# Gathering the experts' tokens in fp32 from the plain norm, one expert and then pairs

## The chip, the cores and the metric

The kernel runs on one core of one Trainium2 chip. The metric is the device time of one execution in microseconds (us); the median of several runs is quoted. Engines are named as in the profile: PE is the matrix engine (TensorE), PEld its weight loads, DVE the vector engine, ACT the scalar engine, POOL GpSimd, and SP the engine that issues the DMAs here.

## The reference

Two decoder layers on 256 tokens of width 2048, in float32. The part that the change touches is the last one: a layer norm, and after it a mixture of eight SwiGLU experts, of which each token takes two.

```python
h = layer_norm(DN_ALPHA * h + mixed @ odd_w_out[i], odd_ln1_g[i], odd_ln1_b[i])
h = layer_norm(DN_ALPHA * h + moe_swiglu(h, odd_router[i], odd_moe_w_gu[i], odd_moe_w_down[i]),
               odd_ln2_g[i], odd_ln2_b[i])

def moe_swiglu(x, w_router, w_gu, w_down):
    ...
    top_vals, top_idx = lax.top_k(logits, TOP_K)
    top_w = jax.nn.softmax(top_vals, axis=-1)
    gates = jnp.sum(jax.nn.one_hot(top_idx, N_EXPERTS, dtype=jnp.float32) * top_w[..., None], axis=1)
    y = jnp.zeros(xt.shape, jnp.float32)
    for e in range(N_EXPERTS):
        y = y + gates[:, e:e + 1] * swiglu(xt, w_gu[e], w_down[e])
```

## The kernel before

Tokens are two tiles of 128 (t = 0, 1), channels 16 blocks of 128 (KC) or 4 blocks of 512 (NCB). A large matmul is made of three matmuls in fp32r (`mm3`, L116 to L118): a value is split into its fp32r rounding (`h`, hi) and the remainder (`l`, lo), and hi by hi, hi by lo and lo by hi are added in PSUM. Weights come in groups of 4 channel blocks, 1 MB each (`load`): SP issues the DMA into `raw` (5 buffers), ACT casts it to `wh` (L107), DVE subtracts for `wl` (L108); `wh` and `wl` have 4 buffers each. `self.plan` gives a `wl` an instruction of DVE that it has to come behind.

The matmuls of one output block are `block`/`blocks`. After each two channel blocks they call `step_fill`, which takes one entry from the list `self.fill` and issues it.

`moe` follows the output projection of the odd layer (`out_proj`), which leaves alpha * h + f(h) in `self.h[t]` and its statistics. It makes 1/std and mean (`rstd`, `nmr`), router logits, the two largest (`top2`, L782 is the selection `sel`), and a slot number for each chosen token and expert (`pos1`, L681) by a triangular matmul over `sel` (L679 to L698). A few matmuls without a use (`keep_busy`, L900) lie between.

Tile t = 0 of h is normed on DVE (`ln_apply`, L224 and L225). Tile t = 1 is normed on ACT (L659) and multiplied by g and shifted by b on DVE (L673, L674, L688, L689). Then `token_parts` splits both into `xth` (ACT, L634) and `xtl` (DVE, L635).

An expert's tokens are not indexed but gathered by a matmul with a one-hot matrix `Dt` (token by slot, 128 slots per expert, made by L809 from `pos1`). `gather` makes this for two experts at a time: in four quarters of 4 channel blocks, for the hi and then the lo part, L827 multiplies `xth` or `xtl` (the stationary operand, 128 x 128) by `Dt` (256 columns moving, fp32r), and ACT copies two blocks at a time to `xe` (L829). `slots` (L838) adds the transposed `Dt` and the gate of each slot.

For each expert `expert_up` runs six blocks of 16 channel blocks (widths 512, 512, 512, 512, 384, 384), with SwiGLU and transposes after each pair, and `expert_down` four blocks of 11 channel blocks. Each of those four is followed by the scatter back to the tokens (L886, L887, `DT`) and an add into h (`add_stats`). The first gather, of experts 0 and 1, lies ahead of expert 0. The others lie in the `expert_down` of experts 1, 3 and 5, a quarter (`step(n)`) ahead of each of the four blocks.

The tiles `xth`, `xtl`, `xe` and the rows of g and b (`load_gb`, four tiles) come from one pool of 17 buffers (`punit`, tag "unit"); small PSUM results from 4 buffers (`ps`). The order of instructions on an engine is set when the program is built, by dependencies and by the order in the source among what the builder's own model takes to be ready.

Of the kernel before, what the change touches and what calls it, by code (L numbers as in the profile page):

```python
# [10 lines left out]
F32 = mybir.dt.float32  # L11
# [3 lines left out]
AF = mybir.ActivationFunctionType  # L15
ALU = mybir.AluOpType
AX = mybir.AxisListType

P = 128
D = 2048  # L20
KC = D // P
NT = 2
CB = 512
NCB = D // CB
WINDOWS = (2, 4, 8, 16)
NEXP = 8
# [46 lines left out]
class Trunk:  # L73
# [23 lines left out]
    def load(self, src, w=CB):  # L97

        nc = self.nc
        fence = self.plan.pop(0) if self.plan else None  # L100
        src = src.rearrange("p (k n) -> p k n", n=w)
        kc = src.shape[1]
        raw = self.praw.tile([P, kc, w], F32, tag="raw", name="raw")
        wh = self.pw.tile([P, kc, w], F32R, tag="wh", name="wh")
        wl = self.pw.tile([P, kc, w], F32R, tag="wl", name="wl")
        nc.sync.dma_start(raw, src)
        nc.scalar.copy(wh, raw)  # L107
        self.after(nc.vector.tensor_tensor(wl, raw, wh.bitcast(F32), ALU.subtract), fence)  # L108
        return wh, wl, kc

    def loads(self, src, w=CB):
# [489 lines left out]
    def router_prep(self, pm):  # L601

        nc, i = self.nc, self.i
        self.gR = pm.tile([P, 2, P], F32, tag="Dt", name="gR", bufs=2)[:, 0, :].rearrange("p (k e) -> p k e", k=KC)
        tmp = self.pln.tile([P, KC * (NEXP + 2)], F32, tag="lnT", name="bR")
        bR = tmp[:, :KC * NEXP].rearrange("p (k e) -> p k e", k=KC)
        cols = tmp[:, KC * NEXP:].rearrange("p (a c) -> p a c", a=2)
        red = pm.tile([P, 2 * NEXP], F32, tag="rred", name="rred", bufs=1)
        self.rows = pm.tile([P, 2 * NEXP], F32, tag="rrows", name="rrows", bufs=1)
        nc.sync.dma_start(bR, i["odd_router"].rearrange("p (k e) -> p k e", k=KC))  # L610
        nc.sync.dma_start(cols, i["ln_cols"][:, 4 * KC:].rearrange("p (a c) -> p a c", a=2))
        for a, dst in ((0, self.gR), (1, bR)):
            nc.vector.tensor_tensor(dst, bR, cols[:, a, :].unsqueeze(2).to_broadcast([P, KC, NEXP]), ALU.mult)
            nc.vector.tensor_reduce(red[:, a * NEXP:(a + 1) * NEXP], dst.rearrange("p k e -> p e k"), AX.X, ALU.add)
        ps = self.ps()
        nc.tensor.matmul(ps[:, :2 * NEXP], self.c[:, C_ONE:C_ONE + P], red, start=True, stop=True)
        nc.vector.tensor_copy(self.rows, ps[:, :2 * NEXP])
        self.lg = [self.acc() for _ in range(NT)]
        nc.scalar.preload_act_table_set("natural_log_exp_and_others")
# [9 lines left out]
            nc.tensor.matmul(self.lg[t][:, :NEXP], rT[:, j * P:(j + 1) * P], self.gR[:, k, :],  # L629
                             start=k == 0, stop=k == KC - 1)  # L630

    def token_parts(self, src, dst, q, fence):
        cs = slice(q * CB, (q + 1) * CB)
        self.nc.scalar.copy(dst[0][:, cs], src)  # L634
        self.after(self.nc.vector.tensor_tensor(dst[1][:, cs], src, dst[0][:, cs].bitcast(F32), ALU.subtract), fence)  # L635

    def moe(self, pm, stats, G, B):
        nc, tc, i = self.nc, self.tc, self.i
        xtok = {}
        sel, pos1, gg = {}, {}, {}  # L640
# [3 lines left out]
        mm = nc.tensor.matmul  # L644
        for t in range(NT):
            gg[t] = gall[:, 0:t + 2:t + 1, :]
        for t in range(NT):
            for half in range(2):
                xtok[t, half] = (self.unit("xth", shape=[P, 1024]), self.unit("xtl", shape=[P, 1024]))
        gates = {}  # L650
        for t in range(NT):
            mean, rstd = self.rstd(stats[t])
            if t == 0:
                self.plan += [self.last]
            nmr = self.nmr(mean, rstd)
            hs = [self.h[t][:, n * CB:(n + 1) * CB] for n in range(NCB)]
            if t:
                for n in range(NCB):
                    nc.scalar.activation(hs[n], hs[n], AF.Identity, bias=nmr, scale=rstd)  # L659
            lrow = pm.tile([P, NEXP], F32, tag="lrow", name="lrow", bufs=1)  # L660
            logits = pm.tile([P, NEXP], F32, tag="logits", name="logits", bufs=1)
            nc.vector.scalar_tensor_tensor(lrow, self.rows[:, :NEXP], nmr, self.rows[:, NEXP:],
                                           ALU.mult, ALU.add)
            nc.vector.scalar_tensor_tensor(logits, self.lg[t][:, :NEXP], rstd, lrow, ALU.mult, ALU.add)
            sel[t], gates[t] = self.top2(logits)
            if t == 0:
                for n in range(NCB):
                    self.ln_apply(hs[n], mean, rstd, G[n], B[n])
                h0 = hs
        fence = self.last  # L670
        self.plan += [fence] * 3
        self.keep_busy(8, self.c[:, :CB // 2].bitcast(BF16))
        self.after(nc.vector.tensor_tensor(hs[0], hs[0], G[0], ALU.mult), fence)  # L673
        self.after(nc.vector.tensor_tensor(hs[0], hs[0], B[0], ALU.add), fence)  # L674
        for t in range(NT):
            pp = self.ps()
            if t == 1:
# [3 lines left out]
            ins = nc.vector.scalar_tensor_tensor(pos1[t], pp[:, :NEXP], 1.0, sel[t], ALU.add, ALU.mult)  # L681
            self.after(ins, fence)
        self.keep_busy(6, self.c[:, :CB // 2].bitcast(BF16))
        gat = self.gather(xtok, [pos1[t][:, 0:2] for t in range(NT)], gg, 0, 0)
        fence = self.last
        for n in range(NCB):
            if n:
                self.after(nc.vector.tensor_tensor(hs[n], hs[n], G[n], ALU.mult), fence)  # L688
                self.after(nc.vector.tensor_tensor(hs[n], hs[n], B[n], ALU.add), fence)  # L689
            self.token_parts(h0[n], xtok[0, n // 2], n % 2, fence)  # L690
            self.token_parts(hs[n], xtok[1, n // 2], n % 2, fence)
        for t in range(NT):
            gv = gg[t][:, 1, :2 * NEXP].rearrange("p (e s) -> p e s", s=2)
            nc.scalar.copy(gv[:, :, 0], gates[t])
# [7 lines left out]
        fstats = [self.stats_tile() for _ in range(NT)]  # L702
# [2 lines left out]
        gat[4]()  # L705
        for e in range(NEXP):
            cur = gat
            hT = self.expert_up(e, cur, e % 2)
            step = None
            if e % 2 and e + 1 < NEXP:  # L710
                gat = self.gather(xtok, [pos1[t][:, e + 1:e + 3] for t in range(NT)], gg, e + 1, 0)
                gat[4]()
                step = gat[3]
            self.expert_down(e, cur, e % 2, hT, e == 0, fstats if e == NEXP - 1 else None, step)

        G, B = self.load_gb(i["odd_ln2_g"], i["odd_ln2_b"])
        self.final_norm(fstats, G, B)
        most_v = nc.values_load(most[0:1, 0:1], min_val=0, max_val=2 * P)
        with tc.If(most_v > P):
# [3 lines left out]
            with tc.For_i(0, NEXP) as e:  # L723
                gat = self.gather(xtok, [pr[:, t, 0:1] for t in range(NT)], gg, 0, P, num=1)
# [3 lines left out]
                hT = self.expert_up(e, gat, 0)  # L728
# [67 lines left out]

    def gather(self, xtok, pos, gg, e, offset, num=2):

        nc, pm = self.nc, self.pm
        mm = nc.tensor.matmul  # L800
        Dt = []
# [10 lines left out]
        xe = {}  # L812
        us = {}

        def quarter(q):
            for part in range(2):
                if q % (3 - num) == 0:
                    us[part] = self.unit("xe", shape=[P, (3 - num) * 4, num * P])
                u = us[part][:, q % (3 - num) * 4:q % (3 - num) * 4 + 4, :]
                for r in range(2):  # L820
                    ps = self.ps()
                    for j in range(2):
                        o = ps[:, j * num * P:(j + 1) * num * P]
                        c = q * 4 + r * 2 + j
                        cs = slice((c % 8) * P, (c % 8 + 1) * P)
                        for t in range(NT):
                            mm(o, xtok[t, c // 8][part][:, cs], Dt[t].rearrange("p a b -> p (a b)"),  # L827
                               start=j == 0 and t == 0, stop=t == 1, skip_group_check=True)
                    nc.scalar.copy(u[:, r * 2:r * 2 + 2, :],  # L829
                                   ps[:, :2 * num * P].rearrange("p (c t) -> p c t", c=2))  # L830
                xe[q, part] = u
        DTs, gss = [], []

        def slots():
            for p in range(num):
# [9 lines left out]
                DTs.append(DT)  # L845
                gss.append(gs)
        return xe, DTs, gss, quarter, slots

    def expert_up(self, e, gat, p):
# [170 lines left out]
```

## Time and profile before

| what | value |
|---|---|
| median of 3 runs | 2180.92 us (2180.24 to 2181.5) |
| the profiled execution, its own time | 2179.94 us |
| its span in the trace | 2178.2 us |
| PE busy in the span | 2144.2 us (98%) |
| DVE, ACT busy | 1457.7 us (67%), 1146.9 us (53%) |
| last matmul of the odd output projection starts | 1336.10 us |
| first weight matmul of expert 0 starts | 1359.86 us |

Times of instructions are us from the start of the span. Matmuls are pipelined: the duration that the trace gives for one (390 ns for 512 columns) is longer than the distance from one start to the next (227 ns), and it is the distance that adds up. A row of the timeline that merges n instructions runs from the first start to the last end.

### The profile page before, as it was taken

Reading aid. Unit: us, or ns where it says so; the run is one execution under the profiler, and the core shown is the slowest. Engines: PE = TensorE matmul, PEld = TensorE weight load, DVE = VectorE, ACT = ScalarE, POOL = GpSimd, SP = SyncE. Lnnn points to the kernel's source line nnn. Section 1 sums busy time; section 2 is a strip of 40 time slices with the busy share of each in tenths; the row PEclk is TensorE's granted clock in tenths of the full one; section 3 lists DMA queues with packets and bytes.
Section 4 is the critical chain, followed back from the end, with each engine's and each line's share of the span. In section 5 each row is a group of like instructions: output and inputs, shape, how many; then the busy total and the mean of one; then the engine's idle time right before and its main releaser. Section 6 shows DMA issues by size and latency. Waiting matters only on the chain.

```text
span 2178.2 us, 24443 instructions
## 1 busy us (share of the span) xinstructions
PE 2144.2 (98%) x9956; PEld 1780.5 (82%) x9956; DVE 1457.7 (67%) x1225; ACT 1146.9 (53%) x962; POOL 1.6 (0%) x6
## 2 busy tenths in 40 slices
PE   9999999999999999999999998999999999999996
PEld 7888888888888888888788887888888888888884
DVE  5443566555455654456676457888888888888988
ACT  5445355343333333343643335766766766676664
POOL 0000000000000000000000000000000000000000
PEclk9999999999999999999999999999999999999998
DMA  9543645555464554455554543999999999998995
GB/s 354 210 155 142 238 179 210 199 195 192 158 226 157 215 191 184 184 190 196 213 193 176 212 160 118 333 351 349 334 336 362 343 338 341 349 346 321 372 353 203
DMA packets 82198, 537.80 MB, mean 247 GB/s; under 512 B 9504, under 2 KB 10656, under 8 KB 28192
## 3 DMA queue, kind: packets, MB, share of 16 engines
q1 hardware_dynamic: 82080, 536.18, 66.1%
q8 instruction: 80, 1.31, 0.2%
q14 instruction: 38, 0.31, 0.0%
HBM read 534.04 MB, written 2.10 MB: 246 GB/s over the span
## 4 chain that ended last, share of the span: by engine, by line
PE 94%; DVE 3%; ACT 1%; DMA 1%; issue 1%; SPq 0%; DVEq 0%; ACTq 0%
PE acc L117 29%; PE acc L118 29%; PE acc L116 29%; PE ps L181 2%; PE ps L827 1%; DVE wl L108 1%; PE ps L886 1%; PE ps L887 1%; ACT wh L107 1%; ACT lnT L259 0%; DMA raw<-in_odd_moe_down_dram 0%; PE ps L575 0%; PE acc L629 0%; PE ps L448 0%; DMA raw<-in_odd_moe_gu_dram 0%
## 5 line engine op out<-in xcount | busy, mean ns | idle before, releaser
L108 DVE TENSOR_TENSOR wl<-raw,wh 128x2048 fp32r<-128x2048 f32 (+2 forms) x519 | 1121.2, 2178 | 394.9 <-ACT wh L107 393.7
L107 ACT CAST wh<-raw 128x2048 fp32r<-128x2048 f32 (+2 forms) x519 | 935.2, 1824 | 444.9 <-PE acc L118 410.2
L117 PE MATMUL acc<-wl,xh 128*128 128x512 f32 x928 | 363.1, 391 | 1.1 <-DVE wl L108 1.1
L116 PE MATMUL acc<-wh,xh 128*128 128x512 f32 x928 | 361.4, 390 | 0.1
L118 PE MATMUL acc<-wh,xl 128*128 128x512 f32 x928 | 361.3, 390 | 0.0
L117 PE MATMUL acc<-wl,xe 128*128 128x512 f32 (+1 forms) x768 | 286.6, 373 | 0.1
L118 PE MATMUL acc<-wh,xe 128*128 128x512 f32 (+1 forms) x768 | 285.4, 372 | 0.0
L116 PE MATMUL acc<-wh,xe 128*128 128x512 f32 (+1 forms) x768 | 284.5, 371 | 0.0
L117 PE MATMUL acc<-wl,hTh 128*128 128x512 f32 x704 | 277.9, 395 | 0.7 <-DVE wl L108 0.6
L118 PE MATMUL acc<-wh,hTl 128*128 128x512 f32 x704 | 277.7, 394 | 0.0
L116 PE MATMUL acc<-wh,hTh 128*128 128x512 f32 x704 | 275.9, 392 | 0.0
L117 PEld LDWEIGHTS acc<-wl,xh 128*128 128x128 f32 x928 | 174.2, 188 | 37.1 <-DVE wl L108 1.5
L116 PEld LDWEIGHTS acc<-wh,xh 128*128 128x128 f32 x928 | 174.1, 188 | 37.1 <-ACT xh L174 0.5
L118 PEld LDWEIGHTS acc<-wh,xl 128*128 128x128 f32 x928 | 174.2, 188 | 36.0 <-DVE xl L175 0.2
L117 PEld LDWEIGHTS acc<-wl,xe 128*128 128x128 f32 x768 | 144.2, 188 | 21.9 <-DVE wl L108 1.8
L116 PEld LDWEIGHTS acc<-wh,xe 128*128 128x128 f32 x768 | 144.2, 188 | 20.6
L118 PEld LDWEIGHTS acc<-wh,xe 128*128 128x128 f32 x768 | 144.2, 188 | 19.8
L117 PEld LDWEIGHTS acc<-wl,hTh 128*128 128x128 f32 x704 | 132.3, 188 | 30.9 <-DVE wl L108 2.1
L116 PEld LDWEIGHTS acc<-wh,hTh 128*128 128x128 f32 x704 | 132.3, 188 | 29.6
L118 PEld LDWEIGHTS acc<-wh,hTl 128*128 128x128 f32 x704 | 132.4, 188 | 27.8
L174 ACT CAST hTh<-ps 128x512 fp32r<-128x512 f32 (+1 forms) x46 | 26.2, 569 | 181.2 <-PE ps L181 181.2
L116 PE MATMUL acc<-wh,x0h 128*128 128x512 f32 x256 | 103.7, 408 | 1.9 <-ACT wh L107 1.9
(195 smaller groups left out, 1793.2 us busy)
## 6 DMA issues: line engine op xcount, KB each, us to landing
raw<-in_odd_moe_gu_dram SPq DMA_DIRECT2D x128, 1024.0 KB, 6.4
raw<-in_even_ffn_gu_dram SPq DMA_DIRECT2D x88, 1024.0 KB, 4.8
raw<-in_odd_moe_down_dram SPq DMA_DIRECT2D x64, 1024.0 KB, 7.1
raw<-in_odd_moe_gu_dram SPq DMA_DIRECT2D x64, 768.0 KB, 5.8
raw<-in_even_ffn_down_dram SPq DMA_DIRECT2D x44, 1024.0 KB, 4.8
raw<-in_odd_w_in_dram SPq DMA_DIRECT2D x32, 1024.0 KB, 4.8
raw<-in_even_w_in_dram SPq DMA_DIRECT2D x30, 1024.0 KB, 5.3
raw<-in_odd_moe_down_dram SPq DMA_DIRECT2D x32, 768.0 KB, 6.6
```

The lines of the kernel that those rows point to most:

```text
L107: nc.scalar.copy(wh, raw)
L108: self.after(nc.vector.tensor_tensor(wl, raw, wh.bitcast(F32), ALU.subtract), fence)
L116: mm(acc, xh, wh, start=first, stop=False)
L117: mm(acc, xh, wl, start=False, stop=False)
L118: mm(acc, xl, wh, start=False, stop=last)
L174: self.nc.scalar.copy(hi, src)
L181: self.nc.tensor.transpose(ps[:, j * P:(j + 1) * P], src[:, j * P:(j + 1) * P], self.ident)
L827: mm(o, xtok[t, c // 8][part][:, cs], Dt[t].rearrange("p a b -> p (a b)"), start=j == 0 and t == 0, stop=t == 1, skip_group_check=True)
L886: nc.tensor.matmul(ps, DT[:, t, :], yh, start=True, stop=False)
L887: nc.tensor.matmul(ps, DT[:, t, :], yl, start=False, stop=True)
```

## The change

The norm writes `(h - mean) / std`, without g and b, for both token tiles by ACT into four tiles `xtok` in fp32; the split into hi and lo is gone from there. The gather multiplies these fp32 tiles by `Dt` read as fp32. Its PSUM result (now with channels on partitions) gets g as a per-partition scale and b as a bias in an ACT activation into `f`, and is split there into hi and lo. g and b as columns (`xcols`) stay from `router_prep` on.

The first gather is for expert 0 alone (`num=1`), the next ones for the pairs (1, 2), (3, 4), (5, 6), in the `expert_down` of experts 0, 2 and 4, and the last for expert 7 alone, in that of expert 6. The residual `h = xtok * g + b` is made by DVE inside `expert_up` of expert 0, as 8 entries of `self.fill`, four steps apart.

```diff
@@ load
-        self.after(nc.vector.tensor_tensor(wl, raw, wh.bitcast(F32), ALU.subtract), fence)
+        self.wl_ins = nc.vector.tensor_tensor(wl, raw, wh.bitcast(F32), ALU.subtract)
+        self.after(self.wl_ins, fence)
@@ router_prep
-        cols = tmp[:, KC * NEXP:].rearrange("p (a c) -> p a c", a=2)
+        cols = self.xcols = pm.tile([P, 2, KC], F32, tag="xcols", name="xcols", bufs=1)
@@ moe
-                xtok[t, half] = (self.unit("xth", shape=[P, 1024]), self.unit("xtl", shape=[P, 1024]))
+                xtok[t, half] = self.unit("xtok", F32, [P, 1024])
...
-            if t:
-                for n in range(NCB):
-                    nc.scalar.activation(hs[n], hs[n], AF.Identity, bias=nmr, scale=rstd)
+            for n in range(NCB):
+                nc.scalar.activation(xtok[t, n // 2][:, n % 2 * CB:(n % 2 + 1) * CB],
+                                     self.h[t][:, n * CB:(n + 1) * CB], AF.Identity, bias=nmr, scale=rstd)
...
-            if t == 0:
-                for n in range(NCB):
-                    self.ln_apply(hs[n], mean, rstd, G[n], B[n])
...
-        self.after(nc.vector.tensor_tensor(hs[0], hs[0], G[0], ALU.mult), fence)
-        self.after(nc.vector.tensor_tensor(hs[0], hs[0], B[0], ALU.add), fence)
...
-        gat = self.gather(xtok, [pos1[t][:, 0:2] for t in range(NT)], gg, 0, 0)
-        fence = self.last
+        gat = self.gather(xtok, [pos1[t][:, 0:1] for t in range(NT)], gg, 0, 0, num=1)
+
+        def residual(t, n):
+            hs = self.h[t][:, n * CB:(n + 1) * CB]
+            self.after(nc.vector.tensor_tensor(hs, xtok[t, n // 2][:, n % 2 * CB:(n % 2 + 1) * CB], G[n],
+                                               ALU.mult), self.wl_ins)
+            nc.vector.tensor_tensor(hs, hs, B[n], ALU.add)
+        self.fill = [None] * 6
         for n in range(NCB):
-            if n:
-                self.after(nc.vector.tensor_tensor(hs[n], hs[n], G[n], ALU.mult), fence)
-                self.after(nc.vector.tensor_tensor(hs[n], hs[n], B[n], ALU.add), fence)
-            self.token_parts(h0[n], xtok[0, n // 2], n % 2, fence)
-            self.token_parts(hs[n], xtok[1, n // 2], n % 2, fence)
+            for t in range(NT):
+                self.fill += [partial(residual, t, n), None, None, None]
@@ moe, the loop over experts
-            hT = self.expert_up(e, cur, e % 2)
+            p = (e + 1) % 2 if e else 0
+            hT = self.expert_up(e, cur, p)
+            while self.fill:
+                self.step_fill()
-            if e % 2 and e + 1 < NEXP:
-                gat = self.gather(xtok, [pos1[t][:, e + 1:e + 3] for t in range(NT)], gg, e + 1, 0)
+            if e % 2 == 0 and e + 1 < NEXP:
+                num = min(2, NEXP - 1 - e)
+                gat = self.gather(xtok, [pos1[t][:, e + 1:e + 1 + num] for t in range(NT)], gg, e + 1, 0, num=num)
@@ gather, quarter
+            if q % (3 - num) == 0:
+                for part in range(2):
+                    us[part] = self.unit("xe", shape=[P, (3 - num) * 4, num * P])
+            o = q % (3 - num) * 4
+            per = 4 // num
+            for r in range(num):
+                ps = self.ps().rearrange("p (c t) -> p c t", c=per)
+                f = self.pln.tile([P, per, num * P], F32, tag="lnT", name="xf")
+                for j in range(per):
+                    c = q * 4 + r * per + j
+                    cs = slice((c % 8) * P, (c % 8 + 1) * P)
+                    for t in range(NT):
+                        mm(ps[:, j, :], xtok[t, c // 8][:, cs], Dt[t].rearrange("p a b -> p (a b)").bitcast(F32),
+                           start=j == 0 and t == 0, stop=t == 1, skip_group_check=True)
+                for j in range(per):
+                    c = q * 4 + r * per + j
+                    nc.scalar.activation(f[:, j, :], ps[:, j, :], AF.Identity, bias=self.xcols[:, 1, c:c + 1],
+                                         scale=self.xcols[:, 0, c:c + 1])
+                at = slice(o + r * per, o + r * per + per)
+                self.split_evac(f, us[0][:, at, :], us[1][:, at, :])
             for part in range(2):
-                if q % (3 - num) == 0:
-                    us[part] = self.unit("xe", shape=[P, (3 - num) * 4, num * P])
-                u = us[part][:, q % (3 - num) * 4:q % (3 - num) * 4 + 4, :]
-                for r in range(2):
-                    ps = self.ps()
-                    for j in range(2):
-                        o = ps[:, j * num * P:(j + 1) * num * P]
-                        c = q * 4 + r * 2 + j
-                        cs = slice((c % 8) * P, (c % 8 + 1) * P)
-                        for t in range(NT):
-                            mm(o, xtok[t, c // 8][part][:, cs], Dt[t].rearrange("p a b -> p (a b)"),
-                               start=j == 0 and t == 0, stop=t == 1, skip_group_check=True)
-                    nc.scalar.copy(u[:, r * 2:r * 2 + 2, :],
-                                   ps[:, :2 * num * P].rearrange("p (c t) -> p c t", c=2))
-                xe[q, part] = u
+                xe[q, part] = us[part][:, o:o + 4, :]
```

## Rows read from the trace of the kernel before

**Rows 1.** Busy time by stretch: PE, PEld, DVE, ACT, POOL; PE clock, DMA share, GB/s.

```profile
1360.00:2152.00 792.00, 790.59 (x3759) 669.95 (x3758) 676.45 (x448) 558.11 (x421) 0.00 (x0) 1.00 0.92 344
...
1360.00:1400.00 40.00, 40.00 (x180) 33.06 (x179) 32.02 (x22) 29.26 (x21) 0.00 (x0) 1.00 0.90 326
1500.00:1550.00 50.00, 50.00 (x269) 44.56 (x269) 40.84 (x31) 36.95 (x37) 0.00 (x0) 1.00 0.93 349
1600.00:1650.00 50.00, 50.00 (x245) 43.78 (x244) 44.92 (x32) 34.06 (x27) 0.00 (x0) 1.00 0.96 358
```

**Rows 2.** Timeline of PE ahead of expert 0: start, length, instruction [idle before, releaser].

```profile
1336.10 0.39 PE L118 MATMUL acc<-wh,mxl 128*128 128x512 f32 x1
...
1343.18 0.37 PE L698 MATMUL ps<-sel,c 128*128 128x8 f32 x2
1345.34 2.44 PE L827 MATMUL ps<-Dt,xth 128*128 128x256 f32 x8 [1.79 <-DVE gates L794]
...
1351.72 1.22 PE L827 MATMUL ps<-Dt,xtl 128*128 128x256 f32 x4 [3.09 <-ACT xe L829]
1352.74 1.91 PE L827 MATMUL ps<-Dt,xth 128*128 128x256 f32 x8
...
1355.55 1.12 PE L827 MATMUL ps<-Dt,xth 128*128 128x256 f32 x8
...
1359.86 0.39 PE L116 MATMUL acc<-wh,xe 128*128 128x512 f32 x1
```

**Rows 3.** Matmuls on fp32r and on fp32 operands: count, duration min/median/max in ns.

```profile
L827 PE MATMUL ps<-Dt,xth x128: 277/281/582, 1345.3 to 1954.7; 128*128 128x256 f32 x128
L386 PE MATMUL ps<-qkT x16: 377/377/379, 100.5 to 173.0; 128*128 128x256 f32 x16
L408 PE MATMUL ps<-atta,v x16: 377/378/378, 110.9 to 183.2; 128*128 128x256 f32 x16
L575 PE MATMUL ps<-sguw,sguv x64: 275/275/348, 1138.5 to 1156.6; 128*128 128x128 f32 x64
```

**Rows 4.** Timeline of PE where such fp32 matmuls run, merged.

```profile
110.94 0.59 PE L408 MATMUL ps<-atta,v 128*128 128x256 f32 x2
111.37 0.39 PE L409 MATMUL ps<-atta,v 128*128 128x128 f32 x2
...
1138.49 3.81 PE L575 MATMUL ps<-sguw,sguv 128*128 128x128 f32 x32 [0.26 <-DVE sguv L225]
```

**Rows 5.** Timeline of DVE ahead of expert 0.

```profile
1342.66 0.23 DVE L782 SCALAR_TENSOR_TENSOR sel<-c,idx,oh 128x8 f32<-128x8 f32 x1
...
1343.65 0.69 DVE L674 TENSOR_TENSOR h<-h,gb 128x512 f32<-128x512 f32 x1
...
1344.33 0.15 DVE L681 SCALAR_TENSOR_TENSOR pos<-ps,sel 128x8 f32<-128x8 f32 x1
...
1344.91 0.28 DVE L809 TENSOR_SCALAR Dt<-c,pos 128x128 fp32r<-128x128 f32 x1
...
1346.23 0.69 DVE L688 TENSOR_TENSOR h<-h,gb 128x512 f32<-128x512 f32 x1
1346.84 0.68 DVE L635 TENSOR_TENSOR xtl<-h,xth 128x512 fp32r<-128x512 f32 x1
...
1353.61 2.29 DVE L108 TENSOR_TENSOR wl<-raw,wh 128x2048 fp32r<-128x2048 f32 x1
```

**Rows 6.** Busy time and granted clock in short stretches, columns as in Rows 1.

```profile
10.00:13.00 3.00, 3.00 (x8) 2.09 (x8) 2.70 (x6) 2.34 (x6) 0.00 (x0) 0.50 1.07 412
14.00:17.00 3.00, 3.00 (x15) 2.47 (x14) 2.08 (x3) 1.37 (x3) 0.00 (x0) 1.00 1.02 397
1336.00:1344.00 8.00, 6.07 (x39) 4.07 (x37) 6.57 (x34) 6.61 (x10) 0.00 (x0) 1.00 0.01 3
1348.00:1351.00 3.00, 0.63 (x3) 0.34 (x2) 3.00 (x6) 1.05 (x2) 0.00 (x0) 0.50 0.00 0
1355.00:1360.00 5.00, 5.00 (x43) 5.00 (x43) 5.00 (x4) 5.00 (x11) 0.00 (x0) 1.00 0.62 216
```

**Rows 7.** Timeline of ACT in an earlier norm: scale and bias from PSUM, then cast.

```profile
1057.28 1.83 ACT L259 ACTIVATE lnT<-ps,lncols 128x128 f32<-128x128 f32 x5
1059.00 0.63 ACT L174 CAST xh<-lnT 128x512 fp32r<-128x512 f32 x1
1059.51 1.52 ACT L259 ACTIVATE lnT<-ps,lncols 128x128 f32<-128x128 f32 x4
1060.89 0.65 ACT L174 CAST xh<-lnT 128x512 fp32r<-128x512 f32 x1
```

More of the change, by code (lines that the diff above doesn't have):

```diff
@@ L604, in router_prep @@
         self.gR = pm.tile([P, 2, P], F32, tag="Dt", name="gR", bufs=2)[:, 0, :].rearrange("p (k e) -> p k e", k=KC)
-        tmp = self.pln.tile([P, KC * (NEXP + 2)], F32, tag="lnT", name="bR")
-        bR = tmp[:, :KC * NEXP].rearrange("p (k e) -> p k e", k=KC)
-        cols = tmp[:, KC * NEXP:].rearrange("p (a c) -> p a c", a=2)
+        bR = self.pln.tile([P, KC, NEXP], F32, tag="lnT", name="bR")
+        cols = self.xcols = pm.tile([P, 2, KC], F32, tag="xcols", name="xcols", bufs=1)
         red = pm.tile([P, 2 * NEXP], F32, tag="rred", name="rred", bufs=1)
@@ L630, in router_step @@
                              start=k == 0, stop=k == KC - 1)
[L632 to L635, printed above, removed]
     def moe(self, pm, stats, G, B):
@@ L655, in moe @@
             nmr = self.nmr(mean, rstd)
-            hs = [self.h[t][:, n * CB:(n + 1) * CB] for n in range(NCB)]
-            if t:
-                for n in range(NCB):
-                    nc.scalar.activation(hs[n], hs[n], AF.Identity, bias=nmr, scale=rstd)
+            for n in range(NCB):
+                nc.scalar.activation(xtok[t, n // 2][:, n % 2 * CB:(n % 2 + 1) * CB],
+                                     self.h[t][:, n * CB:(n + 1) * CB], AF.Identity, bias=nmr, scale=rstd)
             lrow = pm.tile([P, NEXP], F32, tag="lrow", name="lrow", bufs=1)
@@ L665, in moe @@
             sel[t], gates[t] = self.top2(logits)
-            if t == 0:
-                for n in range(NCB):
-                    self.ln_apply(hs[n], mean, rstd, G[n], B[n])
-                h0 = hs
         fence = self.last
@@ L707, in moe @@
             cur = gat
-            hT = self.expert_up(e, cur, e % 2)
+            p = (e + 1) % 2 if e else 0
+            hT = self.expert_up(e, cur, p)
+            while self.fill:
+                self.step_fill()
             step = None
-            if e % 2 and e + 1 < NEXP:
-                gat = self.gather(xtok, [pos1[t][:, e + 1:e + 3] for t in range(NT)], gg, e + 1, 0)
+            if e % 2 == 0 and e + 1 < NEXP:
+                num = min(2, NEXP - 1 - e)
+                gat = self.gather(xtok, [pos1[t][:, e + 1:e + 1 + num] for t in range(NT)], gg, e + 1, 0, num=num)
                 gat[4]()
                 step = gat[3]
-            self.expert_down(e, cur, e % 2, hT, e == 0, fstats if e == NEXP - 1 else None, step)
+            self.expert_down(e, cur, p, hT, e == 0, fstats if e == NEXP - 1 else None, step)
         G, B = self.load_gb(i["odd_ln2_g"], i["odd_ln2_b"])
```

## The prediction

> **What bounds the kernel now.** The page gives PE 98% of the span, but an average over stages doesn't say what one stage is worth, so I read three views in this order. First the busy time by stretch over the experts: PE is busy 790.59 of 792 us, while DVE has 676, ACT 558, and the DMA engines a share of 0.92 [rows 1]. So in this stage PE never waits for weights: whatever PE is given to do there more adds to the time nearly one for one, and at most the 1.4 us of idle can be won back. Second the timeline of PE between the output projection and expert 0: the last matmul of the one starts at 1336.10, the first of the other at 1359.86 [rows 2]. This bridge of 23.8 us is the one place where DVE and ACT set the end. Third, inside the bridge, the order of DVE and the granted clock [rows 5, 6]. The change shortens the bridge and alters PE's work in the expert stage; I cost the two separately.
>
> **What one gather costs PE, before.** A pair has 16 channel blocks, 2 token tiles and 2 parts (hi and lo): 64 matmuls of 256 columns in fp32r. Four gathers make 4 x 32 = 128 records for the hi part, and the trace has 128 [rows 3]: one record per matmul. At full clock eight of them take 1.12 us with the last one's 0.28 us tail [rows 2], so the distance is (1.12 - 0.28) / 7 = 0.120 us. A pair costs 64 x 0.120 = 7.7 us; the three gathers inside the expert stage cost 23.0 us.
>
> **What one gather costs PE, after.** The hi and lo parts become one fp32 operand, so the number of matmuls halves to 32 for a pair. But an fp32 matmul isn't one pass here. The attention scores issue L386 once for each of 8 heads, and the trace has 16 records; L408 likewise; L575 is issued 32 times (16 blocks, 2 tiles) and has 64 [rows 3]. So each fp32 matmul runs as two records. And each record is slow by itself: two of L408 at 256 columns start at 110.94 and what follows them at 111.37 [rows 4], so one takes 0.43 / 2 = 0.215 us, against 0.120 in fp32r. At 128 columns 32 records of L575 span 3.81 us: (3.81 - 0.275) / 31 = 0.114 us. A pair in fp32 is therefore 32 x 2 x 0.215 = 13.8 us, and a single expert 32 x 2 x 0.114 = 7.3 us: as much as a pair costs now.
>
> The row shows 0.43 us for 256 columns in fp32 against 0.120 in fp32r, a factor of 3.6 for half the number of matmuls. The Trainium skill, FP8 and Floating Point Precision, section "TensorE Precision Notes", says that true fp32 takes four passes through the array; by four passes at 0.120 a pair would be an estimated 15.4 us, and the change 4.9 us dearer than I have it over three pairs. The row has the duration, so it is used. The page speaks against halving the matmuls by taking fp32, and the row agrees in direction.
>
> **The expert stage.** After: three pairs, 41.3 us, and expert 7 alone, 7.3 us: 48.6. Minus the 23.0 of before: +25.6 us. All of it stands in PE's own queue between weight matmuls, in a stage where PE has 1.4 us of idle [rows 1]. Bounds: 25.6 - 1.4 = 24 if every idle moment is recovered, and 27 if each quarter adds some tenths at its ends.
>
> The other engines in these gathers: ACT now makes, for 512 elements of a PSUM tile, two activations of 256 columns and one cast, where it made two copies. The trace has no 256-column activation with scale and bias; from above, four of 128 and a cast repeat every 1.89 us (the casts at 1059.00 and 1060.89) [rows 7], 15 us for the eight tiles of a gather; from below it is the copies of today, which are part of ACT's 36.95 of 50 us [rows 1]. I take the upper value, as the nearest row. DVE gets 8 subtractions of 0.6 us, 4.8 us, in a stretch where it has 9 of 50 us free [rows 1]. Both are spread over four blocks in which PE gets 6.1 us longer, and the next expert's `xe` is wanted only after them. Cost nothing; if ACT's ceiling did reach PE through the PSUM buffers, up to 1 us per gather.
>
> **The bridge.** Four steps, all from rows.
> 1. `pos` of tile 1 is written at 1344.33, though its matmul ended at 1343.55: DVE was in the two 0.69 us operations on h (L673, L674), which go [rows 2, 5]. With one expert there are two `Dt`, not four, 0.28 us each. First gather matmul at about 1344.2 instead of 1345.34: 1.1 us.
> 2. The 3.09 us stall [rows 2] goes. It sits where `xe` needs buffers: 8 for the split tokens, 8 for `xe` and 4 for g and b are 20 of 17, so ACT had to wait for the residual. After it is 4 + 4 + 4 = 12. The splits (8 casts, 8 subtractions) and the residual that fed them go from the bridge as well [rows 5].
> 3. The gather itself, 64 records: 7.3 us at full clock. But the clock is at half from about 1345 to 1354.5 [rows 6], and eight fp32r matmuls then take 1.91 us, 0.214 apart [rows 2]; half clock doubles the 0.114 to 0.23. How long will it be low? At the kernel's start PE was busy without a break, and a low stretch (10 to 13) was over before 14 [rows 6]; in the bridge it stayed low through a stretch in which PE was busy 0.63 of 3 us. With nothing to stall it, the new gather looks like the first case. I take 4 us low: 4 / 0.23 = 17 records, and 47 x 0.114 = 5.4: 9.4 us, to 1353.6. With the two `slots` matmuls, 0.24: expert 0 starts at 1353.8.
> 4. Evacuation: 1.9 us of ACT per quarter [rows 7] and a subtraction of 0.69. Quarter 0 is through PE by about 1347.8 and in `xe` by 1351, the last by 1357; expert 0 wants the first at 1353.8 and the last 3 x 12 x 0.227 = 8.2 us later. Hidden.
>
> Gain: 1359.86 - 1353.8 = 6.1 us. Bounds: never low, 1344.2 + 7.3 + 0.24 = 1351.7, a gain of 8.1. Low throughout, 64 x 0.23 = 14.7, gain 0.7; and the builder may put one `wl` (2.29 us, [rows 5]) into the hole that L673 and L674 leave ahead of `pos`, -2.2. So -1.5 to +8.
>
> **The residual in expert 0.** 16 operations on DVE, 0.6 us apart [rows 5], 9.6 us in the roughly 60 us of `expert_up`. DVE is busy 32 of the first 40 us there, so 8 in 40, 12 in 60, are free [rows 1]: that is the cover. Each pair of blocks queues behind the last `wl` issued, and what is behind it on DVE is the next `wl`, for which PE would wait; the weights are three groups ahead, so 1.2 or 2.4 us of delay are bridged. I put it at 0. If the cover is gone (in the fullest stretch DVE has 44.92 of 50), up to 3 us.
>
> Without effect: the norm of tile 0, which moves from DVE to ACT under the matmuls of the output projection; `xcols`; SP's queue, on which no DMA changes its place.
>
> **Sum.** Span 2178.2 + 25.6 - 6.1 = 2197.7. The profiled run's own time is 1.7 above its span, so 2199.4, and the median of the runs shown is 1.0 above that run: 2200.4 us, +0.9%.
>
> **Rivals.**
> - Faster: the gather's fp32 matmul costs one record, not two. Then the expert stage has 3 x 32 x 0.215 + 32 x 0.114 = 24.3 us for 23.0, and the bridge's gather takes about 5: expert 0 starts near 1350.5 (bounded by the first evacuation), 9 us gained: 2180.9 + 1.3 - 9 = 2173. For it: the trace of before has no fp32 matmul with this one-hot operand, which is written as fp32r and only read as fp32. Against: three different fp32 matmuls all show double records. It decides the sign where a 256-column fp32 matmul costs under about 0.27 us (3.5 x 32 x 0.27 = 30, the 23.0 of before and 7 of the bridge). 4%.
> - Faster: the weight stream is the real limit of the expert stage (DMA share 0.96, 358 GB/s in the fullest stretch [rows 1]), and the longer gathers fill waiting time. Then only the bridge counts: 2180.9 - 6.1 = 2175. Against: PE's 1.4 us idle of 792. 3%.
> - The bridge isn't shortened (low clock throughout and a `wl` in front) and the residual makes PE wait: 2180.9 + 25.6 + 0 to 1.5 + 0 to 3 = 2206.5 to 2211. For it: the order on DVE is the builder's, and the clock did stay low for 10 us. 15%.
>
> **How the numbers follow.** The forecast has 78%: 2200.4. Its own range is 24 to 27 for the stage less 8 to 1.5 for the bridge: 2197 to 2206. Taking in the lower part of the third rival, and 1 us for the idle won back: 2196 to 2208. This kernel's measurement tells 0.2% (4.4 us) from no change. Slower by more than that: forecast and third rival, 93%. Within it: 2%, a forecast in which half of the stage's cost is hidden. Faster: 5%.
>
> **What would show it.** The gather's matmul with 192 records at 256 columns and 128 at 128 columns, 0.215 and 0.114 us apart. Four quarters of 3.4 us in the `expert_down` of 0, 2 and 4. First weight matmul of expert 0 near 1353.8, and no stall on `xe`. PE idle in the expert stage still about 1 us. The prediction is wrong if the records aren't double, if PE has gaps that the gathers fill, or if DVE shows up as a releaser of weight matmuls in expert 0.

## The result, and the profile after

The changed kernel takes 2197.97 us (median; 2197.52 to 2198.81), the kernel before 2181.11 us (2180.24 to 2181.94) in the same comparison. The ratio is 1.008, its 95% interval 1.0069 to 1.009: 16.9 us slower. The span of the profiled execution grew from 2178.2 to 2195.6 us, by 17.4.

Part 1 of the page, busy time by engine:

```profile
PE 2167.0 (99%) x10019; PEld 1798.6 (82%) x10020; DVE 1475.2 (67%) x1249; ACT 1169.7 (53%) x1006; POOL 1.6 (0%) x6
```

Busy time by stretch, with columns as in [rows 1]:

```profile
1360.00:2152.00 792.00, 791.96 (x3719) 671.70 (x3718) 681.85 (x470) 570.46 (x455) 0.00 (x0) 1.00 0.90 335
1360.00:1400.00 40.00, 40.00 (x187) 33.77 (x186) 39.15 (x31) 29.76 (x20) 0.00 (x0) 1.00 0.86 312
1336.00:1344.00 8.00, 6.66 (x41) 4.59 (x40) 6.02 (x30) 7.28 (x10) 0.00 (x0) 1.00 0.01 3
1344.00:1351.00 7.00, 6.95 (x62) 6.98 (x63) 7.00 (x10) 4.82 (x13) 0.00 (x0) 1.00 0.49 183
```

In the same 792 us PE is idle for 0.04 us where it was idle for 1.4 [rows 1], and it does less: the DMA engines move 335 GB/s where they moved 344, since the weights are used more slowly. PE was the limit and still is. In the first 40 us DVE is busy 39.15 us, where it was 32.02 [rows 1]: the residual. In the last stretch, the gather, the granted clock is 1.00, where it was 0.50 [rows 6].

The timeline of PE, first the bridge, which answers [rows 2], then a quarter of a later gather and the last matmuls of all, the scatter of expert 7:

```profile
1336.75 0.39 PE L119 MATMUL acc<-wh,mxl 128*128 128x512 f32 x1
...
1344.05 7.38 PE L824 MATMUL ps<-Dt,xtok 128*128 128x128 f32 x64 [0.32 <-DVE Dt L805]
...
1351.39 0.39 PE L117 MATMUL acc<-wh,xe 128*128 128x512 f32 x1
...
1415.88 3.62 PE L824 MATMUL ps<-Dt,xtok 128*128 128x256 f32 x16
...
2175.54 0.74 PE L889 MATMUL ps<-yl,DT 128*128 128x512 f32 x2
```

In the kernel before, the scatter of expert 7 ends with this row:

```profile
2158.02 0.74 PE L887 MATMUL ps<-yl,DT 128*128 128x512 f32 x2
```

The bridge, from the last matmul of the output projection to the first weight matmul of expert 0, is now 1351.39 - 1336.75 = 14.64 us, where it was 23.76: a gain of 9.1. The gather has no break in it, and the stalls of 1.79 and 3.09 us [rows 2] are gone.

The gather's matmul as a group (count of records, duration min/median/max in ns, first and last start, then the shapes; the counts beside them, 96 and 64, are here those of the matmuls that the kernel issues), which answers [rows 3]:

```profile
L824 PE MATMUL ps<-Dt,xtok x320: 270/378/380, 1344.1 to 2069.5; 128*128 128x256 f32 x96, 128*128 128x128 f32 x64
```

There are 320 records for 160 matmuls (3 x 32 for the pairs, 2 x 32 for experts 0 and 7): two for each, at both shapes. At 256 columns 16 records span 3.62 us, so they lie (3.62 - 0.378) / 15 = 0.216 us apart; at 128 columns 64 span 7.38, so (7.38 - 0.275) / 63 = 0.113. The expert stage is taken here from the start of the first weight matmul of expert 0 to the start of the last matmul of expert 7's scatter. It is 824.5 us, where it was 798.5: it grew by 26.0 us.

DVE in the bridge and after it, which answers [rows 5]:

```profile
1342.84 0.23 DVE L777 SCALAR_TENSOR_TENSOR sel<-c,idx,oh 128x8 f32<-128x8 f32 x1
...
1343.55 0.17 DVE L669 SCALAR_TENSOR_TENSOR pos<-ps,sel 128x8 f32<-128x8 f32 x1 [0.27 <-PE ps L667]
1343.63 0.47 DVE L805 TENSOR_SCALAR Dt<-c,pos 128x128 fp32r<-128x128 f32 x2
1344.10 2.28 DVE L108 TENSOR_TENSOR wl<-raw,wh 128x2048 fp32r<-128x2048 f32 x1
1346.36 2.28 DVE L108 TENSOR_TENSOR wl<-raw,wh 128x2048 fp32r<-128x2048 f32 x1
1348.63 0.67 DVE L176 TENSOR_TENSOR xe<-xf,xe 128x512 fp32r<-128x512 f32 x1
...
1364.67 2.29 DVE L108 TENSOR_TENSOR wl<-raw,wh 128x2048 fp32r<-128x2048 f32 x1 [0.42 <-ACT wh L107]
1366.88 1.29 DVE L676 TENSOR_TENSOR h<-xtok,gb 128x512 f32<-128x512 f32 x2
1368.08 1.29 DVE L678 TENSOR_TENSOR h<-h,gb 128x512 f32<-128x512 f32 x2
1369.29 4.49 DVE L108 TENSOR_TENSOR wl<-raw,wh 128x2048 fp32r<-128x2048 f32 x2
```

`pos` of tile 1 now follows its matmul at once, and two `wl` stand directly behind `Dt`; before, the first `wl` in the bridge stood at 1353.61, behind the operations on h [rows 5]. The residual's four operations at 1366.88 lie between two `wl`, inside expert 0. The page's list of waits has PE's weight loads waiting for `wl` for 4.9 us in the whole span, where it was 6.2 us before, and PE is busy 40.00 of the first 40 us of expert 0: the residual made nobody wait.

So the sum of the trace is 26.0 - 9.1 = 16.9 us, and 0.65 us by which the output projection happened to end later (1336.75 for 1336.10): 17.5 us, where the span grew by 17.4.

### The profile page after: what moved, and what is told of

The parts are those of the page before. It is cut to its first block, busy times and chain, and to the rows that moved or that the text cites. A ratio compares the mean times of both kernels' runs of the same rounds, so it can differ in the third digit from the quotient of the medians.

```text
span 2195.6 us, 24656 instructions
## 1 busy us (share of the span) xinstructions
PE 2167.0 (99%) x10019; PEld 1798.6 (82%) x10020; DVE 1475.2 (67%) x1249; ACT 1169.7 (53%) x1006; POOL 1.6 (0%) x6
## 4 chain that ended last, share of the span: by engine, by line
PE 96%; DVE 2%; ACT 1%; issue 0%; DMA 0%; SPq 0%; DVEq 0%
PE acc L118 29%; PE acc L119 29%; PE acc L117 29%; PE ps L824 3%; PE ps L182 2%; DVE wl L108 1%; PE ps L888 1%; PE ps L889 1%; ACT lnT L260 0%; PE ps L576 0%; PE ps L449 0%; PE acc L629 0%; DMA raw<-in_even_w_in_dram 0%; PE ps L399 0%; DVE h L235 0%
```

## The experiments

**Theory.** The change is two things. The bridge gets 9 us shorter because nothing in it waits for the norm's g and b any more; and each gather of a pair gets 6 us longer, because an fp32 matmul of 256 columns runs as two records of 0.216 us where the fp32r pair of matmuls took 0.120 each. **Rivals.** The longer stage comes from something else that came with the change (the odd pairing, two activations for each tile on ACT, the residual on DVE); or the shorter bridge comes from the single-expert gather alone.

**The later gathers in fp32r.** All but expert 0's gather multiply a token operand in fp32r, in as many matmuls as before. Here the high part is multiplied twice and the low part is left out, so the gathered tokens come out about doubled; the number of matmuls is that of a real split, but DVE's subtractions for a low part are not made.

```diff
+    nc.scalar.copy(self.hi[key][:, cs], xtok[key][:, cs])            # in residual
...
-    mm(ps[:, j, :], xtok[t, c // 8][:, cs], Dt[t]....bitcast(F32), ...)
+    for part in range(2):
+        mm(ps[:, j, :], hi[t, c // 8][:, cs], Dt[t]..., ...)
```

> The changed kernel with all gathers behind the first one taken back to fp32r: ACT also casts the plain norm into hi tiles inside expert 0, and a gather multiplies hi twice where hi and lo would stand (the low parts are left out of the gathered tokens, so their cost is there and their value is not). Grouping, evacuation with g and b, and residual stay. Theory (fp32 operands cost two records of 0.215 us each at 256 columns, and nothing else in the change costs PE time among the experts): each of three pairs falls from 64 x 0.215 = 13.8 to 64 x 0.120 = 7.7 us, the single stays at 7.3; 2198.0 - 18.3 = 2179.7, between 2178 and 2182. Rival (the longer evacuation on ACT and DVE, the residual, or the extra gather for expert 7 is the cost): 2192 or more.

Measured: 2179.89 us (2178.33 to 2183.18), ratio to the kernel before 0.9998 (0.9989 to 1.0008). The timeline of PE in this kernel, a pair and expert 7 alone:

```profile
1425.41 2.04 PE L836 MATMUL ps<-Dt,xth 128*128 128x256 f32 x16
...
2040.09 1.45 PE L836 MATMUL ps<-Dt,xth 128*128 128x128 f32 x12
```

The same 16 records that span 3.62 us in fp32 span 2.04 in fp32r: (2.04 - 0.280) / 15 = 0.117 us apart. The bridge is 14.64 us, as in the changed kernel, and the expert stage 806.6: 17.9 us less than in the changed kernel, and 8.1 more than before. That is the theory's number. Taken the other way: the odd pairing, ACT's activations and the residual are all still in this kernel, and together they cost 8.1 us, of which some 7.2 (64 x 0.112) is the eighth expert's own gather. So what the eighth expert's own gather costs is nearly what the bridge gives back, and the fp32 pairs are the loss.

**Pairs from expert 0 on, in fp32.** Four gathers of pairs as before, the first in the bridge again.

```diff
-    gat = self.gather(xtok, [pos1[t][:, 0:1] for t in range(NT)], gg, 0, 0, num=1)
+    gat = self.gather(xtok, [pos1[t][:, 0:2] for t in range(NT)], gg, 0, 0)
...
-    if e % 2 == 0 and e + 1 < NEXP:
+    if e % 2 and e + 1 < NEXP:
```

> The changed kernel with the grouping of before: pairs (0,1), (2,3), (4,5), (6,7), all in fp32. Theory: the gather ahead of expert 0 grows from 7.1 to 13.8 us (+6.6), the expert stage loses the gather of expert 7 alone (-7.3): 2197.3, between 2195 and 2199. Rival A (starting with one expert is what shortens the bridge, as the evacuation of a pair, up to 15 us of ACT, holds expert 0 up): 2203 or more. Rival B (the fp32 gathers among the experts are partly hidden, so that moving one ahead of expert 0 costs its full price and saves less): 2200 to 2204.

Measured: 2197.49 us, ratio 1.0078 (1.0061 to 1.0095), no different from the changed kernel. PE's timeline:

```profile
1337.21 0.39 PE L119 MATMUL acc<-wh,mxl 128*128 128x512 f32 x1
...
1344.71 14.05 PE L823 MATMUL ps<-Dt,xtok 128*128 128x256 f32 x64 [0.52 <-DVE Dt L804]
...
1359.07 0.39 PE L117 MATMUL acc<-wh,xe 128*128 128x512 f32 x1
```

A whole pair in fp32 in the bridge is 64 records in 14.05 us, against 64 in 7.38 for one expert. The bridge is 21.86 us, 7.2 longer than after, and the stage 816.6, 7.9 shorter. A gather of one expert ahead only moves 7 us from the bridge into the stage: at these two widths PE pays for fp32 by the column (0.113 us a record at 128, 0.216 at 256), and eight experts have the same columns however they are grouped. The bridge with the whole fp32 pair is only 1.9 us shorter than that of the kernel before (21.86 against 23.76). So 7.2 of the 9.1 us gained there are the second expert's gather put off to the stage, and the rival of the single expert holds for that part. The waits and the low clock that are gone pay for the dearer fp32 gather of a pair and 1.9 us more.

**The residual ahead of expert 0.** The sixteen operations of the residual are issued before expert 0, not inside it.

```diff
-    self.fill = [None] * 6
+    self.wl_ins = self.last
     for n in range(NCB):
         for t in range(NT):
-            self.fill += [partial(residual, t, n), None, None, None]
+            residual(t, n)
```

> The changed kernel with the residual made ahead of expert 0, right behind the one-hot matrices, instead of inside expert 0. Theory (inside expert 0 the residual is covered by DVE's free time and costs nothing; ahead of it, 16 x 0.6 = 9.6 us of DVE stand in front of the low weights and the low parts of the first gather): 2200 to 2206. Rival (the residual inside expert 0 makes PE wait): 2197 or less.

Measured: 2202.52 us, ratio 1.0102 (1.0085 to 1.0118), 4.6 us more than the changed kernel. PE's and DVE's timelines, then two windows:

```profile
1352.75 0.38 PE L840 MATMUL ps<-gg,Dt 128*128 128x256 f32 x1 [1.70 <-DVE gg L686]
...
1354.03 0.79 PE L119 MATMUL acc<-wh,xe 128*128 128x512 f32 x1 [0.89 <-DVE xe L176]
```

```profile
1352.69 0.68 DVE L678 TENSOR_TENSOR h<-h,gb 128x512 f32<-128x512 f32 x1
1353.29 1.29 DVE L176 TENSOR_TENSOR xe<-xf,xe 128x512 fp32r<-128x512 f32 x2
```

```profile
1350.00:1354.00 4.00, 1.43 (x9) 0.80 (x7) 4.00 (x10) 0.37 (x1) 0.00 (x0) 0.95 0.00 0
1354.00:1357.00 3.00, 2.97 (x7) 2.39 (x8) 3.00 (x4) 2.99 (x9) 0.00 (x0) 0.50 0.00 0
```

The bridge by its definition is still 14.64 us, but PE then stands: for `gg` 1.70 us, for `xe` 0.89, both behind the residual on DVE, which is busy 4.00 of 4 us while PE is busy 1.43. Behind that idle stretch the granted clock is 0.50. The stage is 829.1 us, 4.6 longer. So moving the residual is worth 4.6 us of the change, which is about half of the bridge's gain, and inside expert 0 it costs nothing. A shorter bridge as the first weight matmul shows it isn't yet a gain: one has to see that the next one follows.

**Without the filler matmuls.** The two stretches of `keep_busy` matmuls in the routing part are left out.

```diff
-    self.keep_busy(8, self.c[:, :CB // 2].bitcast(BF16))
...
-    self.keep_busy(6, self.c[:, :CB // 2].bitcast(BF16))
```

> The changed kernel without the two batches of matmuls without a use (8 and 6) between the router and the gather. Theory (they keep the clock at full, and a half clock would stretch the first gather from 7.1 us towards 14 us): 2201 to 2205, granted clock 0.5 for part of the gather. Rival (without stalls the gather itself keeps or brings back the clock): 2197 to 2199.

Measured: 2200.38 us (2198.47 to 2201.38), ratio 1.0091 (1.0074 to 1.0108): 2.4 us more than the changed kernel, 0.6 below what the theory gave and over 1 above the rival. Its four executions are scattered, and the lowest lies among those of the changed kernel (2197.52 to 2198.81), so the trace is the firmer evidence. One row of PE's timeline and three windows:

```profile
1343.86 9.18 PE L822 MATMUL ps<-Dt,xtok 128*128 128x128 f32 x64
```

```profile
1336.00:1344.00 8.00, 4.19 (x27) 3.48 (x26) 6.05 (x32) 6.92 (x8) 0.00 (x0) 0.80 0.01 3
1344.00:1347.00 3.00, 3.00 (x15) 3.00 (x16) 3.00 (x3) 0.00 (x0) 0.00 (x0) 0.50 0.00 0
1348.00:1351.00 3.00, 3.00 (x30) 3.00 (x29) 1.68 (x6) 2.97 (x9) 0.00 (x0) 1.00 0.93 393
```

Without the fillers PE is busy 4.19 of the 8 us ahead of the gather, where it was 6.66, and the clock is at its lower level (1.2 of 2.4 GHz) from about 1340.8 on: a mean of 0.80 over 8 us is 3.2 us at half. PE gets through 15 matmuls in 3 us there and 30 in 3 us after it. The gather takes 9.18 us, not 7.38, so about 3.6 us of it (the 1.8 us more, doubled) are at half. The bridge is 16.65 us, 2.0 longer. So both were half right: without the fillers the clock does fall and costs the bridge 2 us, as the theory has it, and the gather does bring it back, as the rival has it, but only after about 3.6 us. The theory's 2201 was 0.6 us high, as the low stretch ended that early.

**The kernel before, its gather read as fp32.** No part of the change but the way the operands are read: same matmuls, same buffers, same residual.

```diff
-    mm(o, xtok[t, c // 8][part][:, cs], Dt[t]..., ...)
+    mm(o, xtok[t, c // 8][part][:, cs].bitcast(F32), Dt[t]....bitcast(F32), ...)
```

> The kernel before with one thing changed: the gather's operands, the hi and lo tiles and the one-hot matrix, are read as fp32 instead of fp32r. Number of matmuls, columns, grouping and everything else stay. Theory (an fp32 matmul is two records, 0.215 us each at 256 columns): a pair takes 64 x 0.43 = 27.5 instead of 7.7 us, +19.8 for each of the three pairs among the experts, and the first one, 14 us with its stalls, takes at least 27.5, +13 to +20; 2181 + 59 + 13 to 20 = 2253 to 2260; the records of the gather's matmul double. Rival (fp32 costs the gather one record of 0.215): +6.1 for each of three and +3 to +6 for the first: 2202 to 2206.

Measured: 2257.0 us, ratio 1.0347 (1.0329 to 1.0366). The group of the high part's matmul, and one of its rows in PE's timeline:

```profile
L827 PE MATMUL ps<-Dt,xth x256: 377/379/765, 1346.8 to 2028.3; 128*128 128x256 f32 x128
...
1355.24 3.62 PE L827 MATMUL ps<-Dt,xth 128*128 128x256 f32 x16
```

The same 128 instructions that had 128 records [rows 3] have 256, and they are 0.216 us apart. The stage is 59.9 us longer: three gathers of 64 matmuls, each 2 x 0.216 - 0.120 = 0.312 dearer, make 3 x 64 x 0.312 = 59.9. The bridge is 15.1 longer, not 20.0 as 64 x 0.312 would give: the stall of 3.09 us [rows 2] is gone under the longer gather, and the low stretch of the clock is shorter there (the granted clock is 1.00 from 1350 on, where it was 0.50 until about 1354.5). The price of fp32 in this place is thereby measured by itself. The Trainium skill, FP8 and Floating Point Precision, section "TensorE Precision Notes", has true fp32 at four passes; four times the 0.120 us of fp32r would be an estimated 0.480. The rows have 0.432, 3.6 times: near it at this width, and in two records. The ratio doesn't count passes, though: at 128 columns it is 0.226 to 0.112, 2.0 times, since fp32r hardly gets cheaper there (see the last section).

**Can the short bridge be had without fp32?** Pairs again, the plain norm split into high and low part in fp32r, g and b as columns in the evacuation as in the changed kernel, residual inside expert 0. The rows of g and b for the residual have to stand somewhere; here they take two of the buffers in which the raw weights land.

```diff
+    def load_gb_raw(self, g, b): ...                  # two tiles of praw
+    def split(t, fence=None): ...                     # hi: ACT cast, lo: DVE subtraction
-    nc.scalar.activation(xtok[t, n // 2][...], self.h[t][...], AF.Identity, bias=nmr, scale=rstd)
+    nc.scalar.activation(hs, hs, AF.Identity, bias=nmr, scale=rstd)
...
-    mm(ps[:, j, :], xtok[t, c // 8][:, cs], Dt[t]....bitcast(F32), ...)
+    mm(ps[:, j, :], xtok[t, c // 8][part][:, cs], Dt[t]..., ...)      # part 0, 1
```

> A version that keeps what shortens the bridge and drops fp32: hi and lo of the plain norm, gathered in fp32r in pairs from (0,1) on as before, g and b as columns at the evacuation, residual inside expert 0 from the plain norm left in h. The rows of g and b stand in two of the five weight landing buffers until the residual is done, as the tiles would not fit otherwise. Theory (bridge 23.8 us in the kernel before and 14.4 in the changed one; here the gather is 64 x 0.120 = 7.7 us behind about 1 us of waiting for the low parts of tile 1, and four PSUM buffers may hold it up by 1 to 2 us; expert stage as before): 2180.9 - 7.5 = 2173.5, between 2171 and 2177. Rival (two landing buffers fewer, or the longer evacuation of pairs, make PE wait for weights): 2178 or more.

Measured: 2187.14 us, ratio 1.0032 (1.002 to 1.0044): a miss. The list of waits (total us, times, longest) and a window:

```profile
ACT wh L107 <- DMA raw<-in_odd_moe_gu_dram: 24.9, 21, 3.3
...
PEld acc L118 <- DVE wl L108: 19.8, 25, 2.0
...
1360.00:1450.00 90.00, 80.49 (x365) 65.17 (x365) 75.71 (x61) 60.06 (x47) 0.00 (x0) 1.00 0.81 304
```

The first weight matmul comes 15.0 us after the output projection, as hoped, but the bridge isn't over with it: 24 of the gather's 64 matmuls and 4 of `slots` come behind it, 3.3 us. And ACT waits 24.9 us for weights to land, where it was 1.3 us in the kernel before, and PE is idle for 9.5 of 90 us. The weights were to be ahead by as many groups as there are landing buffers, and two of those were lent out.

**The landing buffers given back.** The rows of g and b rotate through two small tiles, loaded in part inside expert 0.

```diff
-    def load_gb_raw(self, g, b): ...
+    def load_gb_row(self, n): ...                     # a unit [P, 2, CB]: row n of g and of b
...
+    self.fill[25] = partial(self.load_gb_row, 2)
+    self.fill[33] = partial(self.load_gb_row, 3)
...
-    self.punit = e(self.pool("units", 17))
+    self.punit = e(self.pool("units", 18))
```

> The version before it with the two weight landing buffers given back: the rows of g and b stand in two tiles of the pool, one for each 512 channels, the third and fourth loaded when the residual has freed the first and second; the pool has 18 tiles instead of 17, and g and b as columns lie in a tile of the earlier norms, which is free by then. Theory (in the version before it the bridge was 15.0 us and PE waited some 12 us for weights because the landing buffers were short): those waits fall to 1 to 4 us, 2187.1 - 10 = 2177, between 2174 and 2180. Rival (the waits come from DVE, which has the pair's subtractions, the low parts and the residual on top of the weights): 2184 or more.

Measured: 2179.32 us (2177.42 to 2182.19), ratio 0.9995 (0.9986 to 1.0004): inside the range, at its upper end, and no difference from the kernel before that can be measured. Waits, a window and rows of ACT, PE and DVE:

```profile
PEld acc L118 <- DVE wl L108: 10.5, 17, 1.9
ACT wh L107 <- DMA raw<-in_odd_moe_gu_dram: 8.2, 11, 1.9
...
1360.00:1450.00 90.00, 86.74 (x397) 72.82 (x397) 81.94 (x66) 63.43 (x50) 0.00 (x0) 0.98 0.85 319
...
1363.47 3.73 ACT L107 CAST wh<-raw 128x2048 fp32r<-128x2048 f32 x2
...
1352.38 0.39 PE L117 MATMUL acc<-wh,xe 128*128 128x512 f32 x1
...
1356.80 0.63 PE L845 MATMUL ps<-Dt,xtl 128*128 128x256 f32 x4
...
1367.78 0.50 PE L118 MATMUL acc<-wl,xe 128*128 128x512 f32 x1 [0.73 <-DVE wl L108]
...
1415.58 1.29 DVE L697 TENSOR_TENSOR h<-h,gb 128x512 f32<-128x512 f32 x2
...
1419.64 4.49 DVE L108 TENSOR_TENSOR wl<-raw,wh 128x2048 fp32r<-128x2048 f32 x2
...
1421.98 0.64 PE L118 MATMUL acc<-wl,hTh 128*128 128x512 f32 x1 [1.66 <-DVE wl L108]
```

The lent buffers were the larger part: PE's idle time fell from 9.5 to 3.3 us in these 90. The stage is 806.8 us, 8.3 longer than before, and three things make up most of it. The gather reaches into the stage as in the version before it: its last matmuls start at 1356.80, behind the first weight matmul at 1352.38, 3.3 us with `slots`. PE is idle for 4.1 of the 792 us after 1360, where it was 1.4 [rows 1]: 2.7 more. And the granted clock, 0.98 on average over these 90 us, was at half for about 3.6 of them, an estimated 1.8 us.

Of the idle time, 0.73 us at 1367.78 is close behind ACT's late cast of weights. That cast starts at 1363.47, behind the evacuation of a whole pair, where it starts at 1354.69 in the changed kernel; in the kernel before it starts at 1362.82, but there expert 0 starts only at 1359.86. The longest wait, 1.66 us at 1421.98, is for a `wl` at 1419.64 that stands on DVE behind four operations of the residual (from 1415.58) and a `silu`. So the rival, DVE, isn't out for what is left; no run took either of the two away. None of the versions here beats the kernel before by a measurable amount.

## Why the prediction held, and where it was off

The forecast was 2200.4 us, the time is 2197.97. By its steps:

- **What one fp32 matmul costs.** 0.215 and 0.114 us for a record and two records for each matmul, read from the attention and the spatial gate [rows 3, 4]; the trace has 0.216, 0.113, and 320 records. Right, and the kernel before read as fp32 confirms it without the rest of the change. The rival of single records is out.
- **The expert stage.** +25.6 forecast, +26.0 measured, inside 24 to 27. PE idle was forecast at about 1 us and is 0.04, so the 1.4 us of [rows 1] were mostly filled, and the quarters cost a little at their ends; neither size was separated: the gathers by their measured distances make 25.7 of the 26.0, and what filled the idle time has no row here. The rival by which the weight stream hides the longer gathers is out: with fp32r instead of fp32 17.9 us of the stage go away.
- **The bridge: the term that was mis-sized.** A gain of 6.1 us was forecast, with 8 as the upper bound, and 9.1 is measured, outside the bounds. Two parts of its working failed. The larger is the clock in step 3: 4 us at half were assumed, so 9.4 us for the gather and 0.24 for the `slots` matmuls; the granted clock was 1.00 throughout, and it took 7.34 us from the gather to expert 0, 2.3 less. The smaller is step 1: the gather was to start 8.1 us after the last matmul of the output projection and started 7.30 after it, 0.8 less. About 0.5 of that is `sel`, which came 6.1 us after that matmul, where it came 6.6 before [rows 2, 5], and the rest is the shorter way from there through `pos` and `Dt`. The "never low" bound had the clock right and the start wrong, which is why 8 was too little. At its other end the term has a slip: the bounds of the gain are worked out as -1.5 to +8, but the range is added up with a gain of at least 1.5. With -1.5 it would reach to about 2209 instead of 2206; the time lies near the lower end, so nothing hung on it.
- **Why the clock stayed up.** Before, PE stood idle for 1.79 us ahead of the gather [rows 2], and two windows of the kernel before have the granted clock at 0.98 and then 0.68 on average:

```profile
1335.00:1345.00 10.00, 7.07 (x43) 4.91 (x41) 7.96 (x44) 7.59 (x11) 0.00 (x0) 0.98 0.02 6
1345.00:1360.00 15.00, 11.54 (x69) 10.99 (x70) 15.00 (x24) 11.37 (x23) 0.00 (x0) 0.68 0.21 72
```

  So it was at half from about 1344.6 to 1354.6. After, PE stood for 0.32 us and the clock stayed. Leaving out the fillers in the changed kernel brought the low clock back, with a gather of 9.18 us, close to the 9.4 of step 3. So the price of 4 us at half was worked out rightly and put where it didn't occur. That the shorter idle is what kept the clock agrees with these rows, but no run changed the idle alone. Nor does it take one long gap: in the version with the lent buffers PE stood for 0.64, 0.52 and 0.35 us around the start of the gather, and the clock was 0.66 on average from 1345 to 1350.
- **The stall for buffers** (step 2) is gone, as forecast, and evacuation is hidden (step 4). That the 3.09 us came from a lack of buffers was not tested: before, ACT's first copies to `xe`, for which PE waited, stand behind a cast to `xth` that waits for DVE, and that order would be enough for the stall.

```profile
1350.57 0.62 ACT L634 CAST xth<-h 128x512 fp32r<-128x512 f32 x1 [1.79 <-DVE h L689]
1351.09 1.55 ACT L829 CAST xe<-ps 128x512 fp32r<-128x512 f32 x3
```

- **The residual at nothing in expert 0.** Right: the cover named, DVE's free 8 of 40 us [rows 1], shows as 39.15 of 40 busy, and no weight load waits longer. With the residual ahead of expert 0 it costs 4.6 us. The rival in which the bridge isn't shortened and DVE makes PE wait is out.
- **ACT with two activations and a cast** for each tile was put at up to 1.89 us and hidden. The rows shown are those of the fp32 pair in the bridge (the second experiment), whose tiles have the same shape:

```profile
1355.65 1.02 ACT L827 ACTIVATE xf<-ps,xcols 128x256 f32<-128x256 f32 x2
1356.70 0.62 ACT L175 CAST xe<-xf 128x512 fp32r<-128x512 f32 x1
1357.22 1.02 ACT L827 ACTIVATE xf<-ps,xcols 128x256 f32<-128x256 f32 x2
```

  One tile repeats after 1357.22 - 1355.65 = 1.57 us, under the 1.89 taken. That the stage's three pairs hid it follows from PE's idle time of 0.04 us.

The span was forecast at 2197.7 and is 2195.6. The difference is -2.1: +0.4 from the stage, -3.0 from the bridge, +0.65 from the output projection's end. The sign came from one comparison, 25.6 against at most 8, and no error in the bridge could have turned it. That the time stayed inside the range although the bridge's gain left its bounds is in part luck: the stage came out above its forecast, and the output projection ended 0.65 us later.

## What to carry to other kernels

Halving the number of matmuls by joining a high and a low part is no saving if the joined operand is fp32: look for other fp32 matmuls in the same trace, count their records against their instructions, and take their distance at the width that is wanted. Price a change stage by stage: 9 us won where PE waits for others stood against 26 us of added work where PE never waits. A buffer lent for a moment can be the depth of a stream: the version that gave two landing buffers back was 7.8 us faster (2187.14 to 2179.32) than the one that lent them.

## What the runs showed that was not expected

At 128 columns fp32r matmuls and the records of fp32 matmuls are equally far apart: 12 in 1.45 us in the run with fp32r gathers, the last of them 0.22 long, make 0.112 us, against 0.113. At 256 columns they are 0.117 to 0.120 and 0.216. In fp32r a gather for one expert therefore costs PE nearly as much as one for two (64 matmuls, 7.2 us against 7.7), and in fp32 with 32 matmuls it costs the same again, 7.3 us: at 128 columns the joined fp32 operand is free against the split in two, at 256 columns it costs 1.8 times the split. The choice of one expert for the bridge hit the one of the two widths measured at which fp32 loses nothing; the three pairs after it lost 6 us each.
